# Float16 pairs in place of float32r pairs for the feed-forward and for attention's queries and keys

## The chip, the cores and the metric

The kernel runs on one core of a Trainium2 chip. The metric is the device time of one execution in microseconds (us). The kernel before took 3118.67 us (median of three runs, 3118.27 to 3121.66). One more execution was recorded by the hardware profiler; it took 3119.8 us, and the span from its first to its last instruction is 3117.9 us.

## The reference

One layer of a diffusion transformer, in float32, over 2048 tokens of width 1024, with 256 context tokens. Cut to its core:

```python
h  = modulate(rmsnorm(x,  norm1_g), sh1,  sc1)       # 2048 x 1024
hc = modulate(rmsnorm(xc, norm1_g), csh1, csc1)      # 256 x 1024
rq, rk, rv, rg, aq, ak, av = split(h @ w_in)         # widths 512 512 512 512 512 128 128
ret = ret_out(bidir_retention(rope(rq), rope(rk), rv), rg)           # 4 heads, chunks of 128
q = rope(rmsnorm(aq, q_norm_g)); k = rope(rmsnorm(ak, k_norm_g))     # 8 query heads, 2 key heads, width 64
att = softmax(q @ [k_ctx, k].T * 64**-0.5) @ [v_ctx, v]              # 2304 keys
x = x + g1 * (concat[ret, att] @ w_out)
h2 = modulate(rmsnorm(x, norm2_g), sh2, sc2)
x = x + g2 * (square(relu(h2 @ w_ff1)) @ w_ff2)      # 1024 -> 4096 -> 1024
out = rmsnorm(x, final_norm_g)
```

The shifts, scales and gates (`sh1`, `sc1`, `g1`, `sh2`, `sc2`, `g2`) are the six parts of `silu(c) @ w_mod + b_mod`.

## The kernel before, in words

Tiles have 128 partitions. Engines: PE multiplies, and PEld loads PE's stationary operand; DVE (VectorE), ACT (ScalarE) and POOL (GpSimd) compute; SP issues most DMAs. PE's wide products are made as pairs: an operand is split into a high part and a low part (`hi = cast(x)`, `lo = x - hi`), and a product is three matmuls (hi hi, hi lo, lo hi) into one PSUM bank. Before the change nearly all pairs are in float32r, a 4-byte form; the softmax numerators (`phi`, `plo`) and the values (`wv`) are in float16.

**First stage** (the `with ExitStack() as st` block). The 18 tiles of tokens go through in three groups of six; for each group six column chunks of `w_in` are multiplied (`products`, L690 to L692). Beside it run the modulation (`w_mod` is read; L306 and `later_rows`, L338 and L340), the rotary embeddings and norms of queries and keys (`post`), and stores of all results to DRAM scratch. Here Tile's scheduler sets the order of the instructions on each engine; an engine then runs its own list strictly in that order. SP's list holds nearly all loads and stores of the stage. A tile pool with `bufs=n` holds n buffers, so load number n + 1 of that pool waits until the first buffer has been read. Near the end `first_maximum` begins the first attention group (PE `mp`, DVE `nm`).

**Attention** (`Group`, run by `attention`) is under an order written out by hand: a table of events by step and phase. There are 32 groups (16 tiles of 128 queries, two key heads, four query heads each), and 18 steps for each, one per 128 keys. In a step PE makes the scores `st` (L179 with the high parts of the queries, L180 with the low parts and two extra rows that carry minus the row's maximum), one piece of the next group's maxima `mp` (L143, L147), and every second step 16 products with the values (`o`, L212 and L213). DVE takes the maxima (`nm`, L156), ACT the exponential (`p`, L185) and its float16 cast (`phi`, L189), DVE or POOL the low part (`plo`). Queries come from the scratch `aq` as float32 and are copied to float32r by ACT (L130, L133). Steps have room on PE beside that: up to about 1030 us the **retention** runs there, afterwards the **output projection** (L1146 to L1148) and the second norm.

**Feed-forward** (from about 1660 us). Two halves of 1024 tokens; for each half 16 blocks of 256 hidden units. A block makes `pu` (L1348 to L1350), squares its relu (`up_out`), and adds `pd` (L1365 to L1367) into `acc` (L1368). `w1` and `w2` come by DMA, `w2` is multiplied by the gate `g2b` on POOL (L1318), and both are split by ACT (L64) and DVE (L65).

Of the kernel before, what the change touches and what calls it, by code (L numbers as in the profile page):

```python
# [11 lines left out]
F32 = mybir.dt.float32  # L12
# [10 lines left out]
P = 128  # L23
# [13 lines left out]
PSHIFT = 8  # L37
VW = 2 * HD + 1
# [14 lines left out]
def layer_kernel(ctx: ExitStack, tc: tile.TileContext, a: dict, out: bass.AP):  # L53
# [12 lines left out]

    half = const.tile([P, 8], F32, name="half")
# [10 lines left out]
    def scratch(name, n, shape):  # L78
        return [dram.tile(shape, F32, name=f"{name}{i}", tag=f"{name}{i}") for i in range(n)]
# [4 lines left out]
    aq_d = scratch("aq", NT, [P, 2, 4, P])  # L84
# [5 lines left out]
    vm_d = dram.tile([P], F32, name="vm", tag="vm")  # L90
    h2_d = scratch("h2", NT, [P, KT, P])
# [7 lines left out]

    keep = ctx.enter_context(ExitStack())  # L100
    kp = keep.enter_context(tc.tile_pool(name="kp", bufs=1, reuse_waits="tile"))
    ks = kp.tile([P, 2, NK * P], F32R, name="ks")
# [9 lines left out]
    class Group:  # L112
# [7 lines left out]
        def load(self, pool=None, tag="q32", bufs=1):  # L120
            self.q = (pool or qp).tile([P, 2, 4, P], F32, name="q32", tag=tag, bufs=bufs)
            for e in range(2):
                src = aq_d[self.t][64 * e : 64 * e + 64, :, 2 * self.g : 2 * self.g + 2]
                q = self.q.rearrange("p x (j e) t -> p x j e t", e=2)
                nc.sync.dma_start(q[:64, :, :, e], src)
                nc.sync.dma_start(q[64:, 0, :, e], src[:, 0])

        def convert(self, pool=None, tag="qr", bufs=3):
            self.qr = (pool or qp).tile([P, 2, 4, P], F32R, name="qr", tag=tag, bufs=bufs)
            nc.scalar.activation(self.qr[:, 0], self.q[:, 0], AF.Copy)  # L130

        def convert_low(self):
            nc.scalar.activation(self.qr[:64, 1], self.q[:64, 1], AF.Copy)  # L133
# [35 lines left out]
        def rows(self):  # L169
            nc.scalar.activation(self.qr[64:, 1], self.m[64:], AF.Copy)  # L170

        def rows2(self):
            nc.vector.tensor_tensor(self.qr[96:, 1], self.m[96:], f32(self.qr[96:, 1]), op=ALU.subtract)
# [8 lines left out]
        def exp(self, kt):  # L182
            if kt % 2 == 0:
                self.p[kt // 2] = pp.tile([P, 2, 512], F32, name="p32", tag="p32")
            nc.scalar.activation(self.p[kt // 2][:, kt % 2], self.s.pop(kt), AF.Exp, bias=shift)  # L185
# [58 lines left out]
    with ExitStack() as st:  # L244
# [203 lines left out]

        def rope(dst, x, c, s, h, d, add_eng):
# [36 lines left out]
        def post(col, kind, i, ps):  # L486
# [39 lines left out]
            elif col == C_AQ:  # L526
# [3 lines left out]
                nc.vector.tensor_scalar_mul(r, r, HD ** -0.5)  # L530
# [5 lines left out]
                def turn(y=y):  # L536
# [3 lines left out]
                    qh = op.tile([P, 4, P], F32R, name="qh", tag="t1")  # L540
                    nc.scalar.activation(qh, pt, AF.Copy)
                    ql = op.tile([P, 4, P], F32, name="ql", tag="t2")
                    nc.vector.tensor_tensor(ql, pt, f32(qh), op=ALU.subtract)
# [1040 lines left out]
```

## Time and profile before

| | |
|---|---|
| time, median of three | 3118.67 us |
| profiled execution: time, span | 3119.8 us, 3117.9 us |
| PE busy, share, matmuls | 2979.0 us, 96%, 17524 |
| DVE busy, share | 1830.9 us, 59% |
| ACT busy, share | 1358.9 us, 44% |
| POOL busy, share | 1267.9 us, 41% |
| HBM read, written | 227.23 MB, 64.10 MB |

A matmul's recorded duration reaches over the starts of its successors, because matmuls are pipelined: a 128x512 matmul is recorded with 390 ns while the next starts 227 ns after it. So PE counts as busy when a matmul is in flight, and what a matmul costs in a dense stream is read from start to start. The granted clock was 0.991 of full speed over the whole span.

### The profile page before, as it was taken

What the parts mean: (1) busy time and instruction counts of PE and PEld (TensorE: products, weight loads), DVE (VectorE), ACT (ScalarE), POOL (GpSimd) and SP (SyncE); (2) the same over time, 40 slices, a digit from 0 to 9 for tenths busy, and PEclk for the clock granted to TensorE, in tenths of its full rate; (3) what the DMA queues carried; (4) which work ended last, traced back from release to release, by engine and by line L of the source; (5) the groups of instructions that cost most, each with busy time, mean ns of one, the idle gap of its engine ahead of it and who ended that gap; (6) DMA issues with size and microseconds to landing.
All of it is one profiled execution on the core that took longest, in us unless ns stands there. A gap on an engine that the chain in (4) does not pass through costs nothing.

```text
span 3117.9 us, 45735 instructions
## 1 busy us (share of the span) xinstructions
PE 2979.0 (96%) x17524; PEld 2419.4 (78%) x17524; DVE 1830.9 (59%) x2939; ACT 1358.9 (44%) x2186; POOL 1267.9 (41%) x1044
## 2 busy tenths in 40 slices
PE   7899998999888899999999999999999999999998
PEld 4787786877776677777777788888887788888886
DVE  4758466368888776677673544444444544444444
ACT  3433244257777777777776222222223222212222
POOL 3547165157777555555555222212224222222222
PEclk9999999999999999999999999999999999999999
DMA  8756544244333221222114311111114311111111
GB/s 265 218 189 194 182 137 134 83 144 141 102 116 92 67 74 63 69 74 69 64 41 161 106 48 49 53 48 43 53 48 138 112 51 51 48 48 48 48 51 54
DMA packets 202611, 294.33 MB, mean 94 GB/s; under 512 B 22932, under 2 KB 104852, under 8 KB 202392
## 3 DMA queue, kind: packets, MB, share of 16 engines
q1 hardware_dynamic: 192112, 283.92, 28.0%
q10 hardware_dynamic: 10280, 7.48, 0.8%
q8 instruction: 138, 2.26, 0.3%
q14 instruction: 81, 0.66, 0.1%
HBM read 227.23 MB, written 64.10 MB: 93 GB/s over the span
## 4 chain that ended last, share of the span: by engine, by line
PE 72%; DVE 9%; POOL 3%; ACT 3%; DMA 3%; issue 2%; SPq 0%; DVEq 0%; ACTq 0%; POOLq 0%
PE pd L1365 7%; PE pd L1367 7%; PE pd L1366 7%; PE pu L1349 7%; PE pu L1348 7%; PE pu L1350 7%; PE st L179 3%; PE st L180 3%; PE mp L143 3%; PE o L213 3%; PE pso L690 2%; PE pso L691 2%; PE pso L692 2%; PE bank L1146 2%; DVE nm L156 2%
## 5 line engine op out<-in xcount | busy, mean ns | idle before, releaser
L1355 POOL TENSOR_TENSOR r<-r 128x512 f32<-128x512 f32 x128 | 134.9, 1054 | 1000.2 <-ACT r L1354 1000.2
L156 DVE TENSOR_REDUCE nm<-mp 128x1 f32<-128x512 f32 (+1 forms) x576 | 393.2, 687 | 228.6 <-PE mp L143 188.4
L185 ACT ACTIVATE p<-st,shift 128x512 f32<-128x512 f32 x576 | 392.8, 689 | 204.7 <-PE st L180 148.7
L1368 DVE TENSOR_TENSOR acc<-pd,acc 128x512 f32<-128x512 f32 x512 | 346.6, 689 | 209.8 <-PE pd L1367 201.9
L196 POOL TENSOR_TENSOR plo<-p,phi 128x1024 f16<-128x1024 f32 x160 | 363.8, 2274 | 255.5 <-ACT phi L189 227.1
L1365 PE MATMUL pd<-w2hi,uhi 128*128 128x512 f32 x1024 | 400.6, 391 | 12.2 <-DVE acc L1368 12.2
L65 DVE TENSOR_TENSOR ulo<-r,uhi 128x512 fp32r<-128x512 f32 x128 | 112.7, 880 | 492.3 <-ACT uhi L64 492.3
L1366 PE MATMUL pd<-w2lo,uhi 128*128 128x512 f32 x1024 | 399.8, 390 | 0.0
L1348 PE MATMUL pu<-h2hi,w1hi 128*128 128x512 f32 x1024 | 398.5, 389 | 1.2 <-ACT h2hi L64 1.2
L1367 PE MATMUL pd<-w2hi,ulo 128*128 128x512 f32 x1024 | 399.5, 390 | 0.0
L1349 PE MATMUL pu<-h2lo,w1hi 128*128 128x512 f32 x1024 | 398.5, 389 | 0.9 <-POOL h2lo L65 0.9
L1350 PE MATMUL pu<-h2hi,w1lo 128*128 128x512 f32 x1024 | 398.3, 389 | 0.0
L64 ACT ACTIVATE w2hi<-ws 128x512 fp32r<-128x512 f32 x128 | 77.8, 630 | 596.1 <-PE pd L1367 521.0
L189 ACT ACTIVATE phi<-p 128x1024 f16<-128x1024 f32 x288 | 303.7, 1054 | 0.0
L690 PE MATMUL pso<-whi,hi_l 128*128 128x512 f32 (+1 forms) x768 | 290.0, 379 | 0.3 <-ACT hi_l L64 0.3
L692 PE MATMUL pso<-whi,lo_l 128*128 128x512 f32 (+1 forms) x768 | 289.2, 377 | 0.1
L691 PE MATMUL pso<-wlo,hi_l 128*128 128x512 f32 (+1 forms) x768 | 289.1, 377 | 0.0
L179 PE MATMUL st<-qr,ks 128*128 128x512 f32 x576 | 266.9, 463 | 1.2 <-ACT p L185 0.6
L143 PE MATMUL mp<-ks,qr 128*128 128x512 f32 x512 | 213.0, 416 | 44.5 <-DVE nm L156 43.7
L213 PE MATMUL o<-wv,phi 128*128 128x129 f16 x2304 | 244.2, 221 | 0.0
L212 PE MATMUL o<-wv,plo 128*128 128x65 f16 x2304 | 238.1, 195 | 3.3 <-DVE plo L198 2.6
L212 PEld LDWEIGHTS <-plo 128*128 128x128 f16 x2304 | 198.7, 98 | 54.6 <-issue 48.0
(317 smaller groups left out, 6009.4 us busy)
## 6 DMA issues: line engine op xcount, KB each, us to landing
ws<-in_w_ff SPq DMA_DIRECT2D x256, 256.0 KB, 2.7
wst<-in_w_in SPq DMA_DIRECT2D x60, 512.0 KB, 4.8
wst<-in_w_mod SPq DMA_DIRECT2D x32, 512.0 KB, 4.8
orv<-rv SPq DMA_DIRECT2D x35, 256.0 KB, 3.0
ork<-rk SPq DMA_DIRECT2D x34, 256.0 KB, 3.4
q<-aq SPq DMA_DIRECT2D x66, 128.0 KB, 3.1
wst<-in_w_mod SPq DMA_DIRECT2D x32, 256.0 KB, 4.4
x_l<-in_x SPq DMA_DIRECT2D x16, 512.0 KB, 6.1
```

Source lines behind the costliest of these rows:

```text
L156: nc.vector.tensor_reduce(dst, src, axis=AX.X, op=ALU.max, negate=True)
L179: mm(ps, ks[:, self.g, k], q[:, 0], start=True, stop=False)
L185: nc.scalar.activation(self.p[kt // 2][:, kt % 2], self.s.pop(kt), AF.Exp, bias=shift)
L196: nc.gpsimd.tensor_tensor(lo, p, hi, op=ALU.subtract)
L212: mm(o[:, : HD + 1], lo[:, i, c], v[:, : HD + 1], start=False, stop=False)
L690: mm(ps[:, :width], hi[:, k], wh, start=k == 0, stop=False)
L1348: mm(ps, whi, hi, start=k == 0, stop=False)
L1349: mm(ps, whi, lo, start=False, stop=False)
L1350: mm(ps, wlo, hi, start=False, stop=k == KT - 1)
L1365: mm(ps, uh, wh, start=f == 0, stop=False)
L1366: mm(ps, uh, wl, start=False, stop=False)
L1367: mm(ps, ul, wh, start=False, stop=f == NF - 1)
```

## The change

It has four parts.

1. The pairs of the feed-forward (`h2`, `w1`, `w2`, `u`) and attention's queries and keys (`qr`, `ks`, `ks2`) become float16. Their matmuls are as many and as large as before; a float16 operand is loaded by a LDWEIGHTS instruction of its own.
2. Powers of two keep the numbers in float16's range. For the feed-forward they come from bounds: `weight_maxima` reads all of `w_ff1` and `w_ff2` (64 tiles of 128x1024) in the first stage and takes the greatest magnitude of each tile on DVE; `ff_scales` combines them over the partitions by way of DRAM and makes the scales, which are folded into `a2` and `s2`, into the splits of `w1` (a scalar on ACT and on DVE), into the relu, into `g2b` and into the addition to `acc`. `binade` cuts a number down to its power of two. For queries and keys `balance` moves a power of two between the two norm weights.
3. The scratch `aq` holds float16, so queries are loaded as they are multiplied, and ACT's two copies for each group are gone.
4. The factor 64**-0.5 and the shift of the exponential, a scalar held in a tile before, move: the factor to the exponential's immediate scale, the shift to a third extra row of the scores.

The diff, cut to its core:

```diff
@@ Group
-        def load(self, pool=None, tag="q32", bufs=1):
-            self.q = (pool or qp).tile([P, 2, 4, P], F32, name="q32", tag=tag, bufs=bufs)
+        def load(self, pool=None, tag="qr", bufs=4):
+            self.qr = (pool or qp).tile([P, 2, 4, P], F16, name="qr", tag=tag, bufs=bufs)
...
-        def convert(self, pool=None, tag="qr", bufs=3):
-            self.qr = (pool or qp).tile([P, 2, 4, P], F32R, name="qr", tag=tag, bufs=bufs)
-            nc.scalar.activation(self.qr[:, 0], self.q[:, 0], AF.Copy)
-
-        def convert_low(self):
-            nc.scalar.activation(self.qr[:64, 1], self.q[:64, 1], AF.Copy)
...
-            nc.scalar.activation(self.p[kt // 2][:, kt % 2], self.s.pop(kt), AF.Exp, bias=shift)
+            nc.scalar.activation(self.p[kt // 2][:, kt % 2], self.s.pop(kt), AF.Exp, scale=HD**-0.5)
@@ first stage
-    ks = kp.tile([P, 2, NK * P], F32R, name="ks")
+    ks = kp.tile([P, 2, NK * P], F16, name="ks")
...
+        def weight_maxima():
+            def piece(i):
+                w = sg.tile([P, D], F32, name="wm", tag="wm", bufs=2)
+                if i < 32:
+                    src = a["w_ff1"][0, i // 4 * P : (i // 4 + 1) * P, i % 4 * D : (i % 4 + 1) * D]
+                else:
+                    src = a["w_ff2"][0, (i - 32) * P : (i - 31) * P, :]
+                nc.sync.dma_start(w, src)
+                nc.vector.tensor_reduce(wmx[:, i : i + 1], w, axis=AX.X, op=ALU.max, apply_absolute_value=True)
+
+            return [lambda i=i: piece(i) for i in range(64)]
+
+        def ff_scales():
+            x = {}
+
+            def spread():
+                w = xp.tile([P, D], F32, name="fs", tag="x", bufs=6)
+                x["m"], m = w[:, 4:516], w[:, :4]
+                nc.vector.tensor_reduce(
+                    m[:, :2], wmx.rearrange("p (a b) -> p a b", a=2), axis=AX.X, op=ALU.max
+                )
...
+                nc.sync.dma_start(sm_d, m)
+                nc.sync.dma_start(
+                    x["m"], sm_d.rearrange("p a -> (p a)").partition_broadcast(P)
+                )
+
+            def scales():
+                b = sm.tile([P, 8], F32, name="fsb", tag="fsb", bufs=1)
...
+            return [spread, scales]
...
+            if (g, c) == (2, 5):
+                spare += ff_scales()
...
+                    if maxima and (g, c) >= (1, 0):
+                        maxima.pop(0)()
@@ feed-forward
         nc.sync.dma_start(ff["g2"], gate_d[1].partition_broadcast(P))
+        m = one.tile([P, 4], F32, name="gm")
+        e, r, k = (m[:, i : i + 1] for i in range(3))
+        nc.vector.tensor_reduce(e, ff["g2"], axis=AX.X, op=ALU.max, apply_absolute_value=True)
+        binade(e)
+        nc.vector.tensor_scalar_mul(e, e, 2.0)
+        nc.vector.reciprocal(r, e)
+        nc.vector.tensor_scalar_mul(r, r, w2s)
+        nc.vector.tensor_scalar_mul(ff["g2"], ff["g2"], r)
+        nc.vector.tensor_tensor(k, sc2, e, op=ALU.mult)
+        ff["k"] = k
...
-            hi = ff["w1"].tile([P, 2, FB], F32R, name="w1hi", tag="w1hi")
-            lo = ff["w1"].tile([P, 2, FB], F32R, name="w1lo", tag="w1lo")
+            hi = ff["w1"].tile([P, 2, FB], F16, name="w1hi", tag="w1hi")
+            lo = ff["w1"].tile([P, 2, FB], F16, name="w1lo", tag="w1lo")
...
-            split(hi, lo, w.rearrange("p (k n) -> p k n", k=2))
+            w = w.rearrange("p (k n) -> p k n", k=2)
+            nc.scalar.activation(hi, w, AF.Copy, scale=sc1)
+            nc.vector.scalar_tensor_tensor(lo, w, sc1, hi, op0=ALU.mult, op1=ALU.subtract)
...
-            [ff["h"].tile([P, KT, 512], F32R, name=f"h2{x}", tag=f"h2{x}{tg}") for x in ("hi", "lo")]
+            [ff["h"].tile([P, KT, 512], F16, name=f"h2{x}", tag=f"h2{x}{tg}") for x in ("hi", "lo")]
...
-        nc.scalar.activation(r, pu.pop((f, tg)), AF.Relu)
+        nc.scalar.activation(r, pu.pop((f, tg)), AF.Relu, scale=scu)
...
-        nc.vector.tensor_tensor(acc[:, c], ps, acc[:, c], op=ALU.add)
+        nc.vector.scalar_tensor_tensor(acc[:, c], ps, ff["k"], acc[:, c], op0=ALU.mult, op1=ALU.add)
```

The scheduler makes a new order of the first stage. Three places are shown; line numbers are those of each kernel's own file.

SP's list in the first stage, before. `wst` are tiles of `w_mod` (L296) and `w_in` (L434), `x_l` tiles of tokens:

```order
L392 DMA x_l_458<-in_x 128x1024
L296 DMA wst<-in_w_mod 128x2x256 x2
L748 DMA n_291<-in_n 128x8
L434 DMA wst<-in_w_in 128x2x512
L296 DMA wst<-in_w_mod 128x2x256 x8
```

The same place after the change, where L312 is the `w_mod` load, L450 the `w_in` load and L656 the new load `wm` of a feed-forward weight tile:

```order
L847 DMA n_297<-in_n 128x8
L656 DMA wm<-in_w_ff 128x1024 x2
L450 DMA wst<-in_w_in 128x2x512
L312 DMA wst<-in_w_mod 128x2x256 x6
L656 DMA wm<-in_w_ff 128x1024 x2
L312 DMA wst<-in_w_mod 128x2x256 x2
```

And the place in the new list where the last of the 64 stands:

```order
L577 DMA aq_124<-qh 128x512
L656 DMA wm<-in_w_ff 128x1024
L450 DMA wst<-in_w_in 128x2x512
L578 DMA aq_124<-ql 128x512
L345 DMA wst<-in_w_mod 128x2x512
L656 DMA wm<-in_w_ff 128x1024
L577 DMA aq_125<-qh 128x512
```

The program text spreads the pieces over the second and third groups; in the list the first two stand ahead of the stage's second `w_in` load, and the last ahead of the store of `aq_125`, a tile of the second group.

DVE's list a little further on, before (rotary embedding of the retention's keys, then the gate's rows of `w_mod`):

```order
L455 TENSOR_TENSOR t_912<-xs,rtb 128x512
L338 TENSOR_SCALAR macc<-wst,cc 128x512
L340 SCALAR_TENSOR_TENSOR macc<-wst,cc,macc 128x512
L462 TENSOR_TENSOR ys<-t_912,t_913 128x512
L340 SCALAR_TENSOR_TENSOR macc<-wst,cc,macc 128x512 x2
L455 TENSOR_TENSOR t_957<-xs,rtb 128x512
```

The same place after, with L657 the maximum of one weight tile:

```order
L489 TENSOR_TENSOR t_902<-xs,rtb 128x512
L657 TENSOR_REDUCE wmx<-wm 128x1
L496 TENSOR_TENSOR ys<-t_902,t_903 128x512
L657 TENSOR_REDUCE wmx<-wm 128x1
L354 TENSOR_SCALAR macc<-wst,cc 128x512
L489 TENSOR_TENSOR t_928<-xs,rtb 128x512
```

Each maximum waits for its load and stands between operations on which ACT and PE depend.

PE's list in a step of attention beside the output projection, before:

```order
L213 MATMUL o_15209<-wv,phi 128x129
L179 MATMUL st<-qr,ks 128x512
L180 MATMUL st<-qr,ks_6226 128x512
L143 MATMUL mp<-ks,qr 128x512
L1146 MATMUL bank_15204<-sf_8485,oat 128x512
```

And after:

```order
L229 MATMUL o_15371<-wv,phi 128x129
L195 LDWEIGHTS ks
L195 MATMUL st<-qr,ks 128x512
L196 LDWEIGHTS ks_6449
L196 MATMUL st<-qr,ks_6449 128x512
L158 LDWEIGHTS qr
L158 MATMUL mp<-ks,qr 128x512
L1250 MATMUL bank_15366<-sf_8689,oat 128x512
```

The matmuls stand in the same order; the float16 ones have their weight loads as rows of their own.

More of the change, by code (lines that the diff above doesn't have):

```diff
@@ L75, in rsqrt, with scratch @@
         return y
-    def scratch(name, n, shape):
-        return [dram.tile(shape, F32, name=f"{name}{i}", tag=f"{name}{i}") for i in range(n)]
+    def scratch(name, n, shape, dtype=F32):
+        return [dram.tile(shape, dtype, name=f"{name}{i}", tag=f"{name}{i}") for i in range(n)]
     rk_d = scratch("rk", NK, [P, 512])
@@ L90, in layer_kernel @@
     vm_d = dram.tile([P], F32, name="vm", tag="vm")
+    sm_d = dram.tile([P, 4], F32, name="smd", tag="smd")
     h2_d = scratch("h2", NT, [P, KT, P])
@@ L447, in layer_kernel, with balance @@
         gnb = one.tile([P, 512], F32, name="gnb")
+        def balance(g):
+            m = sm.tile([P, 4], F32, name="gm", tag="gm", bufs=1)
+            nc.vector.tensor_reduce(
+                m[:, :2], g.rearrange("p a b c -> p a (b c)"), axis=AX.X, op=ALU.max, apply_absolute_value=True
+            )
+            nc.vector.tensor_scalar_max(m[:, :2], m[:, :2], 1e-15)
+            nc.vector.reciprocal(m[:, 2:3], m[:, 0:1])
+            nc.vector.tensor_mul(m[:, 2:3], m[:, 2:3], m[:, 1:2])
+            e = m[:, 2:3].bitcast(I32)
+            nc.vector.tensor_single_scalar(e, e, 24, op=ALU.arith_shift_right)
+            nc.vector.tensor_scalar(e, e, 8388608.0, float(64 << 23), op0=ALU.mult, op1=ALU.add)
+            nc.vector.reciprocal(m[:, 3:4], m[:, 2:3])
+            for i in range(2):
+                nc.vector.tensor_scalar_mul(g[:, i], g[:, i], m[:, 2 + i : 3 + i])
         def rope(dst, x, c, s, h, d, add_eng):
@@ L753, in layer_kernel @@
         mods = mod_steps()
+        maxima = weight_maxima()
         beside = None
@@ L817, in layer_kernel @@
     psX = pool(banks, "psX", space=PSUM, side="right")
-    ks2 = vp.tile([P, 2, NK * P], F32R, name="ks2")
+    ks2 = vp.tile([P, 2, NK * P], F16, name="ks2")
     unit = vp.tile([P, 1], F32, name="unit")
     nc.vector.tensor_tensor(unit, ident[:, 64:65], ident[:, 96:97], op=ALU.add)
-    shift = vp.tile([P, 1], F32, name="shift")
-    nc.vector.memset(shift, PSHIFT * math.log(2.0))
+    nc.vector.tensor_tensor(unit, unit, ident[:, 80:81], op=ALU.add)
+    nc.vector.tensor_scalar_mul(unit, unit, ROW)
     zeros = vp.tile([P, P], F16, name="zeros")
@@ L1334, in make_h @@
         hi, lo = (x[:, 4 * q : 4 * q + 4, j % 4 * P : (j % 4 + 1) * P] for x in ff["hs"][j // 4])
[L1335 removed]
+        split16(hi, lo, ff.pop(("u", i)), eng or (nc.vector if i % 2 else nc.gpsimd))
     UP = [(f, tg) for tg in range(2) for f in range(NF)]
@@ L1353, in up_out @@
         r = ff["r"].tile([P, 512], F32, name="r", tag="r")
-        nc.scalar.activation(r, pu.pop((f, tg)), AF.Relu)
+        nc.scalar.activation(r, pu.pop((f, tg)), AF.Relu, scale=scu)
         nc.gpsimd.tensor_tensor(r, r, r, op=ALU.mult)
-        us[f, tg] = [ff["up"].tile([P, 512], F32R, name=f"u{x}", tag=f"u{x}") for x in ("hi", "lo")]
-        split(*us[f, tg], r)
+        us[f, tg] = [ff["up"].tile([P, 512], F16, name=f"u{x}", tag=f"u{x}") for x in ("hi", "lo")]
+        split16(*us[f, tg], r)
     def down(b, m, n, acc):
```

81 lines of the change are left out of this document (59 added, 22 removed).

## The prediction

> **What bounds the kernel now.** I read the windows first, one per stage (times are from the span's start; 605 to 1030 us is attention beside the retention, 1030 to 1660 us attention beside the output projection, the last is the feed-forward).
>
> ```profile
> core 0: us, PE busy (x) PEld busy (x) DVE busy (x) ACT busy (x) POOL busy (x), PEclk, DMA share, GB/s
> 0.00:29.00 29.00, 13.18 (x49) 3.56 (x50) 6.51 (x16) 9.93 (x17) 6.64 (x18) 1.00 0.92 308
> 29.00:290.00 261.00, 248.99 (x1324) 197.94 (x1323) 183.09 (x305) 96.86 (x177) 138.84 (x162) 0.99 0.64 203
> 605.00:1030.00 425.00, 370.78 (x3149) 305.90 (x3147) 343.81 (x662) 291.11 (x456) 295.94 (x214) 0.98 0.37 117
> 1030.00:1660.00 630.00, 618.51 (x5228) 489.13 (x5227) 435.83 (x739) 502.57 (x757) 323.54 (x218) 1.00 0.19 62
> 1660.00:3118.00 1458.00, 1427.29 (x6338) 1177.13 (x6335) 687.02 (x938) 351.86 (x601) 381.50 (x308) 0.99 0.20 67
> ```
>
> PE is busy 98% of the feed-forward and of the projection's stretch, with the next engine at 47% and 80%. Only beside the retention does PE have time to spare (87%), and DVE is close behind it (81%). PE's waits agree: over 3118 us the longest entries are small.
>
> ```profile
> PE mp L143 <- DVE nm L156: 43.7, 42, 2.6
> PE pd L1365 <- DVE acc L1368: 12.2, 6, 3.8
> ```
>
> Nearly all of the first fall into 605 to 1030 us. So elsewhere the time is the number of matmuls times the distance from one start to the next, and a dearer operation on another engine is free while that engine has room.
>
> **Matmul spacing, the change's main term.** The feed-forward's dense stream, its first and last row of 22 (columns: start, duration, engine, line, operation):
>
> ```profile
> 2201.23 0.39 PE L1365 MATMUL pd<-w2hi,uhi 128*128 128x512 f32 x1
> ...
> 2205.99 0.39 PE L1365 MATMUL pd<-w2hi,uhi 128*128 128x512 f32 x1
> ```
>
> 21 distances in 4.76 us are 226.7 ns for 512 columns. The profile has no wide float16 matmul; the nearest are these, first a block of two with 258 columns, then the first and last of eight pairs with 65 and 129:
>
> ```profile
> 971.17 0.39 PE L204 MATMUL o<-wv,zeros 128*128 128x258 f16 x2
> 971.39 0.19 PE L212 MATMUL o<-wv,plo 128*128 128x65 f16 x1
> ...
> 1304.21 0.22 PE L213 MATMUL o<-wv,phi 128*128 128x129 f16 x1
> ...
> 1304.82 0.22 PE L213 MATMUL o<-wv,phi 128*128 128x129 f16 x1
> ```
>
> Two of 258 columns take 0.22 us, 110 ns each; seven pairs take 0.61 us, 87 ns for 194 columns, or 43.6 ns for a mean of 97. The line through both has (110 − 43.6)/161 = 0.412 ns per column and gives 110 + 254 × 0.412 = 214.7 ns at 512. The float32r rows of 256 columns give another slope:
>
> ```profile
> 80.73 0.28 PE L691 MATMUL pso<-wlo,hi_c 128*128 128x256 f32 x1
> ...
> 82.15 0.28 PE L691 MATMUL pso<-wlo,hi_c 128*128 128x256 f32 x1
> ```
>
> Twelve distances in 1.42 us are 118.3 ns, so (226.7 − 118.3)/256 = 0.423 ns per column, and 110 + 254 × 0.423 = 217.5. I take the middle, 216.5 ns: a float16 matmul saves 10.2 ns, 4.5%. The narrow pairs carry their own weight loads at 44 ns distance, so the added load instructions cost nothing here. Rounding to 10 ns leaves 105 to 115 ns for the 258 columns, hence 211.5 to 221.5 and a saving of 5 to 15 ns.
>
> The feed-forward has 2 × 16 × 64 × 3 = 6144 such matmuls, as this group (one of its six lines, 1024 each) shows:
>
> ```profile
> L1365 PE MATMUL pd<-w2hi,uhi 128*128 128x512 f32 x1024 | 400.6, 391 | 12.2 <-DVE acc L1368 12.2
> ```
>
> 6144 × 10.2 = **−63 us** (bounds −31 to −92). The additions to `acc`, the relu and the splits of `w1` get scalars from tiles. They lie on DVE and ACT: if each of DVE's 938 instructions there took half as long again, DVE would be busy 1031 of 1458 us, so they stay hidden under PE. Without that cover the additions (one row below, 512 of them) at 0.1 us more would cost 51 us.
>
> ```profile
> L1368 DVE TENSOR_TENSOR acc<-pd,acc 128x512 f32<-128x512 f32 x512 | 346.6, 689 | 209.8 <-PE pd L1367 201.9
> ```
>
> The Trainium skill, "TensorE: Matmul & The Clock Gate", section "Wait — 56ns, not 53.3ns?", gives 215.7 ns from start to start for a warm 512-column matmul, which I estimate at 6144 × 11.0 = 68 us saved here, 5 more than my term. The 226.7 ns of this trace are more than that page's figure, and no run here yet shows a wide float16 matmul.
>
> **Attention beside the output projection.** PE is full there, so what it saves is gained. A float32r matmul after a float16 one is dearer: L179 follows the products with the values, L180 follows L179.
>
> ```profile
> L179 PE MATMUL st<-qr,ks 128*128 128x512 f32 x576 | 266.9, 463 | 1.2 <-ACT p L185 0.6
> L180 PE MATMUL st<-qr,ks 128*128 128x512 f32 x576 | 231.1, 401 | 0.0
> ```
>
> The handover is 463 − 401 = 62 ns. After the change the first matmul behind the products is float16 too, and the handover is moved, if it stays, to the projection's matmuls, which already follow maxima or scores. The stretch has this many scores and, in the second row, maxima:
>
> ```profile
> 1030.00:1660.00 630.00, 259.30 (x753) 123.13 (x752) 255.32 (x376) 1.00 0.19 62
> 1030.00:1660.00 630.00, 130.00 (x320) 60.16 (x319) 1.00 0.19 62
> ```
>
> 376 steps × (2 × 10.2 + 62) = 31.0, and 320 × 10.2 = 3.3: **−34 us**. Lower bound of the gain 0 (the handover moves to the projection's matmuls and the spacing stays), upper 40 with 15 ns. I take the sum, since the projection's float32r matmuls come in runs of several, of which a handover meets one.
>
> **Attention beside the retention.** DVE paces it with POOL:
>
> ```profile
> 650.00:1030.00 380.00, 328.72 (x2958) 272.01 (x2958) 331.61 (x641) 276.31 (x434) 283.07 (x202) 0.98 0.39 122
> 650.00:1030.00 380.00, 142.04 (x390) 62.33 (x390) 133.33 (x194) 0.98 0.39 122
> DVE mr L1000 <- POOL cy_gn L863: 24.9, 16, 2.8
> DVE nm L156 <- PE mp L143: 16.2, 19, 1.3
> ```
>
> PE's saving is 194 × 82.4 ns = 16 us, but PE has 51 us idle. DVE waits for PE 16.2 us; a third of that, since its other waits stay, is **−6 us** (bounds 0 and −16).
>
> **ACT in attention.** The exponential no longer reads its shift from a tile, and the copies of the queries go.
>
> ```profile
> L185 ACT ACTIVATE p<-st,shift 128x512 f32<-128x512 f32 x576 | 392.8, 689 | 204.7 <-PE st L180 148.7 <-DVE plo L198 43.6 <-POOL plo L196 9.0
> L522 ACT ACTIVATE xs<-pso 128x512 f32<-128x512 f32 x16 | 9.6, 598 | 37.6 <-PE pso L692 37.5
> L130 ACT ACTIVATE qr<-q 128x512 fp32r<-128x512 f32 x33 | 20.8, 631 | 5.9 <-DMA q<-aq 5.9
> L133 ACT ACTIVATE qr<-q 64x512 fp32r<-64x512 f32 x33 | 20.6, 625 | 0.0
> ```
>
> Up to 576 × (689 − 598) ns = 52 us and 41 us leave ACT. It waits 148.7 us for the scores already, and is idle 127 us beside the projection: **0** (bounds 0 and −16, a shorter chain from scores to products). The float16 queries and keys are written by operations that exist already.
>
> **First stage.** 64 loads of 512 KB and 64 maxima of 128x1024 are added. The nearest maximum and the nearest load, of the same size and rows, and how long that load takes from issue to landing (least, median, most):
>
> ```profile
> L590 DVE TENSOR_REDUCE vma<-vn x3: 937/941/954, 460.8 to 465.3; 128x1 f32<-128x768 f32 x3
> x_l<-in_x SPq DMA_DIRECT2D x16, 512.0 KB, 6.1
> DMA to landing us min/median/max: 3.9/6.0/9.1
> 1698.37 0.14 DVE L1166 TENSOR_TENSOR ss<-ss 128x1 f32<-128x1 f32 x1
> ```
>
> The last row gives a DVE operation's fixed part; 1024 columns take 0.14 + 0.80 × 1024/768 = 1.21 us. In the changed order the pieces stand from the stage's second `w_in` load to just ahead of the store of `aq_125`:
>
> ```profile
> 28.82 0.37 SPq L434 DMA_DIRECT2D wst<-in_w_in  x1
> 282.55 0.32 SPq L544 DMA_DIRECT2D aq<-qh  x1
> ```
>
> so they fall into 29 to 290 us. DVE's busy time there becomes 183.1 + 64 × 1.21 = 260.5 of 261 us. The DMA engines carry 0.64 × 261 = 167 us; 33.6 MB more, at 308/0.92 = 335 GB/s in full use, add 100: 267 of 261 us. Both resources that had room are used up, while every maximum waits for its load and PE waits for DVE's rotary, norm and split operations queued behind it. An engine with such dependences has not run fuller than DVE's 331.6/380 = 87% beside the retention: 260.5/0.87 = 299 us, a stretch of 38; DMA at the 0.92 of the first 29 us gives 290, a stretch of 29. I take **+37 us**, near DVE's. Bounds: 0, if the order fills DVE's gaps, and 77, if every maximum lies on the path. SP's list is one queue, and each `wm` load also holds up the `w_in` and token loads behind it until a buffer is free.
>
> **Small chains.** `ff_scales` stores, reloads and computes on DVE, like the existing round trip: **+3 us** (bounds 0 and 7). Before the feed-forward `g2b` is reduced by eight DVE operations after its landing: **+1 us** (bounds 0 and 5), since PE has projection work left.
>
> ```profile
> DVE vma L599 <- DMA vma<-vm: 6.7, 1, 6.7
> DMA to landing us min/median/max: 5.9/5.9/5.9
> ```
>
> **The sum:** −63 − 34 − 6 + 37 + 3 + 1 = −62, on the profiled 3119.8 us: 3058, and 1.1 less against the median of 3118.67, so **3057 us**.
>
> **Rivals.**
>
> *The maxima hide.* DVE's 78 idle us before the change take 77 us of maxima, and the stage grows by 5 at most: 3057 − 32 = 3025. For it: one scheduler places them by need; against it: DVE would have to run at 98%. The Trainium skill, "DMA: Bandwidth & Descriptors", section "Measured (HBM→SBUF, 128 partitions, SWDGE, issued from GpSimd)", has 425 GB/s for 16 MB; I estimate 79 us for the added bytes by it, which would leave the DMA engines at 246 of 261 us and speak for this rival. No stretch of this trace moves more than 308 GB/s.
>
> *A landing loop, the slower side.* `wm` has two buffers, so two loads, their landing and two maxima make a round, 32 rounds in all, and SP's other loads queue behind them. At 6.1 us of landing a round is 6.1 + 1.2 + 0.7 (two issues) = 8.0 us and 32 make 256, just within the 261. With the DMA engines full the landing will be later: at the longest seen, 9.1 us, they make 352, +91 instead of +37: 3111. From 9.4 us per landing on (361 us) the loss equals the other gains of 99 us; at 10.5 us it is 397, +136: 3156. For it: the sixteen loads took up to 9.1 us at a DMA share of 0.64. Against: not all `wm` loads stand next to other traffic.
>
> *More from attention.* Relieved of the copies and the exponential's scalar, ACT and PE let the retention's steps come sooner, up to the bound of 16 us each beside the 6 counted: −20 more, 3037.
>
> *No gain per wide matmul.* The 226.7 ns could stay, if float16's advantage is one of narrow matmuls. Only the handover is left, 376 × 62 = 23: −23 − 6 + 41 = +12, 3131. Against: the slope per column is the same in both types, so the fixed part is what differs.
>
> **Chances.** Forecast 0.50, maxima hidden 0.22, more from attention 0.12, landing loop 0.12 (two thirds of it slower than before), no gain per wide matmul 0.04. Faster by over 0.2% (6 us, about what a measurement of this kernel can tell): 0.50 + 0.22 + 0.12 and a little of the loop, less the forecast's tail, 0.84; within 0.2% 0.05; slower 0.11. The range reaches from a little under the hidden case, with a spacing 2 ns better than taken (3012), to the loop at 9.1 us (3111).
>
> **What would show it.** Starts of L1365's successors 216 to 217 ns apart in the feed-forward, and that stage 63 us shorter (1395); the mean of the first scores' matmul down by about 60 ns more than the second's; 1030 to 1660 us shorter by 34; DVE above 85% and a DMA share above 0.85 in the first 330 us, the first stage's end (605 us) 37 to 40 us later, and waits of the weight maxima for `wm`. It is wrong if wide float16 matmuls keep 227 ns, if the granted clock in the feed-forward falls (each 0.01 of it is 14 us), if DVE's waits for `wm` exceed 60 us, or if the first stage ends within 10 us of before.

## The result

The changed kernel took 3046.72 us (median of four runs, 3040.09 to 3050.60), beside 3118.84 us for the kernel before on the same chips: a ratio of 0.9765 (95% interval 0.9746 to 0.9783), 72 us or 2.3% faster. The forecast was 3057 us, with a range of 3012 to 3111.

The profiled execution took 3047.53 us, its span is 3045.7. The windows of the profile after, with the boundaries used before (columns: window, length, busy time and count of each engine, granted clock of PE, DMA share, GB/s):

```profile
29.00:290.00 261.00, 244.71 (x1278) 194.36 (x1277) 225.54 (x333) 91.69 (x167) 124.16 (x147) 0.98 0.89 304
290.00:605.00 315.00, 294.92 (x1409) 238.07 (x1408) 192.92 (x323) 109.37 (x184) 135.86 (x135) 0.98 0.49 154
605.00:1030.00 425.00, 364.11 (x3186) 278.21 (x3185) 339.35 (x657) 260.33 (x429) 291.80 (x215) 0.98 0.34 108
1030.00:1660.00 630.00, 606.16 (x5386) 410.13 (x5385) 454.06 (x760) 462.32 (x737) 344.02 (x228) 0.99 0.19 60
1660.00:3045.00 1385.00, 1351.93 (x6224) 615.93 (x6224) 712.87 (x940) 362.48 (x589) 369.22 (x304) 0.99 0.21 70
```

Between 29 and 290 us the DMA share went from 0.64 to 0.89, DVE's busy time from 183 to 226 us, and PE started 46 matmuls fewer in the same time. Between 1030 and 1660 us PE's busy time fell from 619 to 606 us and ACT's from 503 to 462; in the feed-forward PE's fell with the length of the stage and ACT's rose, from 352 to 363 us.

Fixed windows cut a shifted kernel at other places, so the stages are better measured between marks of the program on PE: the last product of the first stage, the first product of the output projection, the feed-forward's first and last matmul. The mark on which most of what follows rests is the last product. Its row before, and then its row after (columns: start, duration, engine, line, operation):

```profile
644.81 0.39 PE L692 MATMUL pso<-whi,lo_l 128*128 128x512 f32 x1
```

```profile
663.03 0.39 PE L791 MATMUL pso<-whi,lo_l 128*128 128x512 f32 x1
```

Lengths in us, from the timelines of the profiled executions (one for each kernel; the changed kernel and the one below with the feed-forward in float32r again have the same program in the first stage, and their marks at its end are 663.0 and 666.5 us, so that a few us between single marks mean nothing):

| | before | after | change | forecast |
|---|---|---|---|---|
| start to the first stage's last product | 644.8 | 663.0 | +18.2 | +37 and +3 |
| from there to the projection's first product (retention) | 401.4 | 395.8 | −5.6 | −6 |
| from there to the feed-forward's first matmul | 645.8 | 621.4 | −24.4 | −34 |
| feed-forward, first to last matmul | 1414.1 | 1353.7 | −60.4 | −63 and +1 |
| rest of the span | 11.8 | 11.8 | 0 | 0 |
| span | 3117.9 | 3045.7 | −72.2 | −62 |

### The profile page after: what moved, and what is told of

The parts are those of the page before. It is cut to its first block, busy times and chain, and to the rows that moved or that the text cites. A ratio compares the mean times of both kernels' runs of the same rounds, so it can differ in the third digit from the quotient of the medians.

```text
span 3045.7 us, 45858 instructions
## 1 busy us (share of the span) xinstructions
PE 2874.4 (94%) x17524; PEld 1740.0 (57%) x17524; DVE 1932.4 (63%) x3035; ACT 1295.5 (43%) x2120; POOL 1271.7 (42%) x1046
## 4 chain that ended last, share of the span: by engine, by line
PE 69%; DVE 14%; DMA 6%; POOL 4%; issue 4%; ACT 2%; SPq 0%; ACTq 0%; DVEq 0%; POOLq 0%
PE pd L1482 7%; PE pd L1484 7%; PE pd L1483 7%; PE pu L1467 7%; PE pu L1465 7%; PE pu L1466 7%; PE o L229 3%; PE st L196 3%; PE st L195 3%; PE mp L158 3%; PE pso L789 3%; DVE nm L171 2%; PE pso L791 2%; PE pso L790 2%; PE bank L1250 2%
## 5 line engine op out<-in xcount | busy, mean ns | idle before, releaser
L1485 DVE SCALAR_TENSOR_TENSOR acc<-pd,gm,acc 128x512 f32<-128x512 f32 x512 | 373.7, 746 | 154.0 <-PE pd L1484 153.8
L201 ACT ACTIVATE p<-st 128x512 f32<-128x512 f32 x576 | 340.7, 598 | 249.2 <-PE st L196 174.5
L1482 PE MATMUL pd<-w2hi,uhi 128*128 128x512 f16 x1024 | 390.0, 381 | 14.1 <-DVE acc L1485 13.9
L1466 PE MATMUL pu<-h2lo,w1hi 128*128 128x512 f16 x1024 | 388.7, 380 | 2.6 <-POOL h2lo L71 2.6
L1465 PE MATMUL pu<-h2hi,w1hi 128*128 128x512 f16 x1024 | 388.9, 380 | 1.2 <-ACT h2hi L70 1.2
L1483 PE MATMUL pd<-w2lo,uhi 128*128 128x512 f16 x1024 | 389.9, 381 | 0.0
L1484 PE MATMUL pd<-w2hi,ulo 128*128 128x512 f16 x1024 | 389.7, 381 | 0.1
L1467 PE MATMUL pu<-h2hi,w1lo 128*128 128x512 f16 x1024 | 388.7, 380 | 0.0
L158 PE MATMUL mp<-ks,qr 128*128 128x512 f16 x512 | 196.7, 384 | 55.8 <-DVE nm L171 55.6
L214 DVE TENSOR_TENSOR plo<-p,phi 128x512 f16<-128x512 f32 x256 | 214.4, 839 | 19.2 <-ACT phi L205 19.1
```

Of the source, the lines that this page charges most:

```text
L1465: mm(ps, whi, hi, start=k == 0, stop=False)
L1466: mm(ps, whi, lo, start=False, stop=False)
L1467: mm(ps, wlo, hi, start=False, stop=k == KT - 1)
L1482: mm(ps, uh, wh, start=f == 0, stop=False)
L1483: mm(ps, uh, wl, start=False, stop=False)
L1484: mm(ps, ul, wh, start=False, stop=f == NF - 1)
```

## Experiments

The time of each kernel is the median of its runs; its ratio is to runs of the kernel before on the same chip. "Last product" is the mark above, read from the profiled execution.

### The feed-forward in float32r again

```diff
-            hi = ff["w1"].tile([P, 2, FB], F16, name="w1hi", tag="w1hi")
+            hi = ff["w1"].tile([P, 2, FB], F32R, name="w1hi", tag="w1hi")
...
-        split16(*us[f, tg], r)
+        split(*us[f, tg], r)
```

and so for `w1lo`, `w2`, `h2` and `u`.

> The changed kernel with the feed-forward's pairs (h2, w1, w2, u) in float32r again; scales, maxima and attention as changed. If the spacing of 216 against 227 ns is the feed-forward's whole gain, its products (first to last) take 1414 us as before the change in place of 1354, and the time is 3047 + 60 = 3107. Rival: a part of it comes from the new order or from DVE and ACT there; then the stage takes 1395 us or less and the time is 3090 or less.

It took 3114.26 us, ratio 0.9974 (0.9965 to 0.9983). The feed-forward's marks lie 1417.6 us apart, 63.9 more than after the change and 3.5 more than before it; the stages ahead of it were as after the change (666.5, 395.1 and 623.9 us). So the feed-forward's operand type is worth 64 us of the 72 and the rest of the change together about 8. The dense stream shows why. After the change, the first and last of 22 rows:

```profile
2200.54 0.38 PE L1465 MATMUL pu<-h2hi,w1hi 128*128 128x512 f16 x1
...
2205.07 0.38 PE L1465 MATMUL pu<-h2hi,w1hi 128*128 128x512 f16 x1
```

21 distances in 4.53 us are 215.7 ns; in float32r they were 226.7. 6144 × 11.0 would be 68 us; 4 to 7 of them went to longer stalls (the longest, for `acc`, 5.6 us).

### The exponential's shift from a tile again

```diff
-            nc.scalar.activation(self.p[kt // 2][:, kt % 2], self.s.pop(kt), AF.Exp, scale=HD**-0.5)
+            nc.scalar.activation(self.p[kt // 2][:, kt % 2], self.s.pop(kt), AF.Exp, scale=HD**-0.5, bias=shift)
```

with the third extra row of the scores left at zero.

> The changed kernel with the shift of the exponential read from a tile again, as before the change, and not in the scores' third row: the mean of the exponential should go from 598 back to 689 ns, 52 us on ACT. By the prediction's step (ACT bounds nothing) the time stays: 3047 within 4 us. Rival: the 7 us gained beside the retention, or a part of the 23 beside the projection, come from the shorter exponential; then 3053 to 3063, with the loss between 668 and 1680 us.

It took 3050.57 us, ratio 0.9773 (0.9759 to 0.9786), which can't be told from the changed kernel's 0.9765. The groups of ACT, first after the change, then in this experiment:

```profile
L201 ACT ACTIVATE p<-st 128x512 f32<-128x512 f32 x576 | 340.7, 598 | 249.2 <-PE st L196 174.5 <-DVE plo L214 60.6 <-POOL plo L212 6.4
```

```profile
L201 ACT ACTIVATE p<-st,shift 128x512 f32<-128x512 f32 x576 | 391.9, 689 | 211.2 <-PE st L196 141.0 <-DVE plo L214 55.4 <-POOL plo L212 8.4
```

The same instruction with the same scale costs 91 ns more for the pointer. Of the 51 us taken from ACT, 38 turn up as idle time ahead of it; the retention's stage (397.7 us) and the projection's (621.3) stay within 2 us of the changed kernel's.

### No maxima

```diff
-        maxima = weight_maxima()
+        maxima = []
+        nc.vector.memset(wmx, 0.25)
```

> The changed kernel without the 64 loads and the 64 maxima of the feed-forward weights; the greatest magnitudes are a constant 0.25 in their place, so that part of the computation is left out. In the changed kernel the last product of the first stage starts at 663.0 us of the span, before the change at 644.8. If the maxima alone stretch the stage, it starts at 643 to 648 us here and the time is 3047 - 18 = 3029 us. Rival: the new order, the scales and the float16 queries and keys cost the 18 us; then it stays at 655 us or later and the time at 3038 or more.

It took 3022.93 us, ratio 0.9683 (0.9670 to 0.9696). The last product:

```profile
639.42 0.39 PE L791 MATMUL pso<-whi,lo_l 128*128 128x512 f32 x1
```

23.6 us ahead of the changed kernel and 5.4 ahead of the kernel before. So the loads and maxima cost some 24 us in the changed kernel, and the other edits of the first stage, or merely the other order that the scheduler finds, gave 5 back (which of the two is not shown).

### Loads alone

```diff
-                nc.vector.tensor_reduce(wmx[:, i : i + 1], w, axis=AX.X, op=ALU.max, apply_absolute_value=True)
+                nc.vector.tensor_reduce(wmj[:, i : i + 1], w[:, :1], axis=AX.X, op=ALU.max, apply_absolute_value=True)
...
+        nc.vector.memset(wmx, 0.25)
```

> The changed kernel with its 64 loads, but each maximum over one column (about 0.14 us, an estimate from a 128x1 operation of the trace, in place of 1.21) and the constant 0.25 for the scales; most of DVE's added 77 us is left out. If DVE's time stretches the first stage (the step of the prediction), the last product starts at 645 to 650 us and the time is about 3031. Rival, the DMA engines (share 0.94 between 29 and 140 us) and SP's one queue: it stays at 658 to 663 us and the time at 3042 to 3047.

It took 3038.73 us, ratio 0.9736 (0.9722 to 0.9749), and the last product starts here:

```profile
657.13 0.39 PE L792 MATMUL pso<-whi,lo_l 128*128 128x512 f32 x1
```

With hardly any of DVE's work, 17.7 of the 23.6 us are still there. This speaks against the step of the prediction that made DVE's pace the cause. It leaves open whether the loads cost by what they carry or by the places where engines wait for them: DVE still stands before loads that have not landed, for 36.2 us in all.

### Maxima alone, and maxima alone but spread

First the maxima over a tile that never changes:

```diff
-                nc.sync.dma_start(w, src)
-                nc.vector.tensor_reduce(wmx[:, i : i + 1], w, axis=AX.X, op=ALU.max, apply_absolute_value=True)
+                nc.vector.tensor_reduce(wmx[:, i : i + 1], wr, axis=AX.X, op=ALU.max, apply_absolute_value=True)
```

> The changed kernel with its 64 maxima of 128x1024 over a tile that lies in the chip's memory and holds 0.25; the 64 loads (33.6 MB) are left out. If DVE's time stretches the first stage, the last product starts at 658 to 663 us and the time is 3042 to 3047. Rival, DMA and SP's queue: 645 to 650 us and about 3031. If both are needed together, both of these halves come out near 648.

It took 3068.45 us, ratio 0.9828 (0.9815 to 0.9841), with the last product at 685.5 us: later than with the loads, which neither theory had. The reason is in the order. With nothing to wait for, the scheduler put all 64 at the head of DVE's list (columns of the second row as in the windows above):

```profile
L655 DVE TENSOR_REDUCE wmx<-wr x64: 1200/1204/1219, 2.9 to 87.0; 128x1 f32<-128x1024 f32 x64
0.00:95.00 95.00, 34.43 (x174) 15.08 (x175) 90.32 (x110) 15.95 (x26) 11.65 (x27) 0.75 0.55 178
```

DVE is busy 90 of the first 95 us, and PE, which waits for the operations queued behind the maxima, 34. The run says nothing on the cause in the changed kernel, only that 64 maxima in one block ahead of everything else cost 46 us against none. So a second form holds each maximum back behind a product of the second or third group:

```diff
-                nc.sync.dma_start(w, src)
-                nc.vector.tensor_reduce(wmx[:, i : i + 1], w, axis=AX.X, op=ALU.max, apply_absolute_value=True)
+                nc.vector.tensor_copy(wr[:, :1], after)
+                nc.vector.tensor_reduce(wmj[:, i : i + 1], wr, axis=AX.X, op=ALU.max, apply_absolute_value=True)
...
-                        maxima.pop(0)()
+                        maxima.pop(0)(ps[:, :1])
```

> The counterpart of the paced kernel without its loads: 64 maxima of 128x1024 over a tile that holds 0.25, each behind a copy of one column of a product of the second or third group, so that they are spread as there (the last product started at 660.0 us) and can't be put ahead of all other work; the scales come from the constant 0.25, and the 33.6 MB are left out. If DVE's added 77 us stretch the stage, the prediction's step, the last product starts at 655 to 661 us and the time is 3038 or more. If the bytes do, it is 641 to 648 us (639.4 without any maxima, and the 6 us that DVE added to the loads) and the time 3024 to 3031.

It took 3016.63 us, ratio 0.9657 (0.9644 to 0.9670): faster than without any maxima. The maxima's group, the last product, and a window in the thick of them:

```profile
L653 DVE TENSOR_REDUCE wmj<-wr 128x1 f32<-128x1024 f32 x64 | 77.6, 1212 | 1.0
632.76 0.39 PE L787 MATMUL pso<-whi,lo_l 128*128 128x512 f32 x1
224.00:330.00 106.00, 102.50 (x506) 82.09 (x505) 101.88 (x160) 38.67 (x69) 64.24 (x71) 1.00 0.60 186
```

DVE's 77.6 us are all there, DVE runs at 96% for 106 us, and PE runs at 97% beside it at full clock. Spread like this, DVE's time by itself stretches nothing. That the stage ends 6.6 us sooner than with no maxima, though it has more work, shows what a new order from the scheduler can do; differences of that size between these kernels are not to be read as costs. The loads' cost stands clear of it: of the kernels with float32r there, this one, the one without maxima and the one that has them elsewhere end the stage at 632.8 to 639.4 us, and the six with all loads in it at 657.1 to 666.5.

### The same spread with loads

```diff
+                nc.vector.tensor_copy(w[:, :1], after)
...
-                    if maxima and (g, c) >= (1, 0):
-                        maxima.pop(0)()
+                    for _ in range(1):
+                        if maxima and (g, c) >= (1, 0):
+                            maxima.pop(0)(ps[:, :1])
```

> The changed kernel with all its work; each of the 64 loads waits for a product of the second or third group (a copy of one column into its tile ahead of the load), one load for each product, so that they are spread from about 225 us to the stage's end and no two come at once by themselves. If the cost is one of density (DMA share of 0.86 to 0.94 for 200 us, in the changed kernel and in the one with late pieces), the last product starts at 645 to 650 us and the time is 3028 to 3034. Rival: the loads cost some 18 us however they are spread: 657 us or later, 3041 or more.

It took 3039.38 us, ratio 0.9735 (0.9722 to 0.9749). The last product, the window above and DVE's longest wait of this kernel:

```profile
659.97 0.39 PE L792 MATMUL pso<-whi,lo_l 128*128 128x512 f32 x1
224.00:330.00 106.00, 98.30 (x487) 78.89 (x486) 97.97 (x158) 38.51 (x67) 66.59 (x70) 0.98 0.78 249
DVE wmx L658 <- DMA wm<-in_w_ff: 57.0, 34, 4.8
```

Against the same spread without loads the stage ends 27 us later, at a DMA share of at most 0.80 in any window of 50 us. Density was not the point: the loads cost about the same spread over 390 us (224.7 to 613.6) as packed into 280. In this form DVE stands before a load that has not landed for 57 us; in the changed kernel for 11.5 us only, but there SP's list stands:

```profile
SPq L656 <- DVE wmx L657: 46.5, 35, 3.0
DVE wmx L657 <- DMA wm<-in_w_ff: 11.5, 11, 2.3
```

### A quarter of the bytes

```diff
-                w = sg.tile([P, D], F32, name="wm", tag="wm", bufs=2)
+                w = sg.tile([P, 256], F32, name="wm", tag="wm", bufs=2)
```

with 256 columns of each weight tile loaded, one column reduced, and the constant 0.25 for the scales as before.

> As the kernel with loads only (64 loads, each maximum over one column, the constant 0.25 for the scales), but each load brings 128x256 in place of 128x1024: 8.4 MB in all, a quarter of the bytes, with the same number of instructions on SP and DVE and the same two buffers. Without loads the last product of the first stage starts at 639.4 us, with full loads at 657.1. If the bytes cost (other loads land later), a quarter of 17.7 is left: 642 to 646 us, 3022.9 + 4 = 3027. Rival, the places in SP's queue and the waits for a free buffer there: 651 to 657 us and 3033 to 3039.

It took 3028.13 us, ratio 0.9702 (0.9689 to 0.9715), and the last product starts here:

```profile
645.60 0.39 PE L792 MATMUL pso<-whi,lo_l 128*128 128x512 f32 x1
```

The same number of instructions on SP and DVE with a quarter of the bytes costs 6.2 us instead of 17.7. The greater part of the loads' cost goes with their bytes, that is, as it seems, with how long they and the transfers beside them take to land; a rest of up to 6 us is queueing, or order. The transfers beside them do land later. The loads of `w_in`, first in the changed kernel, then without loads and maxima (the last number is the median time to landing in us):

```profile
wst<-in_w_in SPq DMA_DIRECT2D x60, 512.0 KB, 5.3
```

```profile
wst<-in_w_in SPq DMA_DIRECT2D x60, 512.0 KB, 4.6
```

It is 5.3 us too with the loads alone, 5.2 with the spread loads, and 4.8 with a quarter of the bytes.

### The maxima at other places

Later in the first stage (the first two loads wait for a product of the second group's third chunk, so that all 64 maxima fall into 296 to 533 us):

```diff
-                    if maxima and (g, c) >= (1, 0):
-                        maxima.pop(0)()
+                    for _ in range(2):
+                        if maxima and (g, c) >= (1, 2):
+                            maxima.pop(0)(ps[:, :1] if len(maxima) > 62 else None)
```

> The changed kernel with all its work; the first two of the 64 loads wait for a product of the second group's third column chunk (a copy of one column into their tile ahead of the load), and the program calls two pieces at each place from there. So the 64 pieces fall into about 300 to 580 us, where the DMA share was 0.45 and DVE busy 55% before the change. If the stretch comes from the place, where both had no room, the last product starts at 646 to 652 us and the time is 3030 to 3036. Rival: the same work costs the same anywhere in the stage: 660 us or later, 3044 or more.

3042.85 us, ratio 0.9749 (0.9735 to 0.9762), last product at 659.1 us: the rival, nearly. And beside the output projection:

```diff
-        maxima = weight_maxima()
+        maxima = []
...
+        for i in range(64):
+            k = 190 + 6 * i
+            on(k, "dma", load, i)
+            on(k + 5, "late", greatest, i, 0)
+            on(k + 5 + 1, "late", greatest, i, 1)
+        on(576, "late", spread)
+        on(576 + 6, "late", scales)
```

> The changed kernel with the 64 loads and maxima taken out of the first stage and put beside the output projection: one load of 512 KB every six steps into one buffer, two maxima of 128x512 behind it, and the weights' scales computed after the last one; the scales of the second norm stay in the first stage. Nothing is left out. The DMA share there is 0.19 and DVE busy 72%. If the bytes cost in the first stage alone because transfers there are awaited, the last product starts at 639 to 642 us, the projection's stretch stays at 621 us and the time is 3023 to 3027. Rival: DVE's 64 x 1.3 us delay the row maxima there and PE waits: the stretch grows to 632 us or more and the time is 3034 or more.

3043.32 us, ratio 0.9749 (0.9736 to 0.9763). The first stage went back to 639.1 us, as without maxima, but the projection's stretch grew from 621.4 to 640.0. The loads landed in good time there (DVE was idle 0.3 us ahead of all 128 maxima), and DVE was busy 82% of the stretch. The maxima's group, and one of ACT's waits in that stretch:

```profile
L1330 DVE TENSOR_REDUCE wmx<-wm 128x1 f32<-128x512 f32 x128 | 86.5, 676 | 0.3
ACT p L203 <- DVE plo L216: 33.5, 20, 2.5
```

The same wait in the changed kernel, over its stretch:

```profile
ACT p L201 <- DVE plo L214: 2.9, 5, 1.7
```

So DVE's later low parts hold up ACT, and ACT the scores. Set matmul for matmul beside the changed kernel, some 11 of the 18.6 us lost come in many small delays on PE up to 1600 us. The other 7 come in the last 77 us of the stretch, where PE waits 8.3 instead of 5.6 us for the second norm (`u`, on DVE) and the granted clock is 0.89 instead of 0.96. The waits point to DVE here; no run separates its time from the loads' bytes. So of three places and one spread, the 64 loads and maxima cost some 19 to 24 us of the stage they stand in.

### More pairs in float16

The first stage's products and the output projection's, unscaled:

```diff
-                hi = hp.tile([P, KT, P], F32R, name=f"hi_{kind}{i}", tag="hhi")
+                hi = hp.tile([P, KT, P], F16, name=f"hi_{kind}{i}", tag="hhi")
...
-            hi = wp.tile([P, 2, 512], F32R, name="whi", tag="whi")
+            hi = wp.tile([P, 2, 512], F16, name="whi", tag="whi")
...
-            x = room_tile(tag, F32R)
+            x = room_tile(tag, F16)
```

> The changed kernel with two more sets of pairs in float16, unscaled: the first stage's products (hidden states and w_in) and the output projection's (w_out times the gate, and what it multiplies). It asks what paces the first stage after the change. The stage has 2064 products of 512 columns and 384 of 256; at 10.6 and about 8 ns less that is 25 us. If PE's spacing paces it, the last product starts near 638 us in place of 663. Rival: the added loads pace it; then it stays at 655 us or later. For the projection the distances of the changed kernel (scores' successor and L1250 to L1251 together 446 ns, 232 and 239 ns behind the others) say 255 x 52 ns = 13 us if every one becomes 216: the stretch from the first projection product to the feed-forward's first goes from 621 to about 608 us. Together 3009 us, by the rival 3026 to 3034.

It took 3012.80 us, ratio 0.9651 (0.9637 to 0.9664), the fastest kernel here that leaves nothing out: another 34 us. The projection's stretch went from 621.4 to 607.7 us, 13.7 less, as worked out from starts (13). The first stage's last product went from 663.0 to 644.7, 18 of the 25 us that the spacing alone would give; by that PE's spacing would still pace a good part of the first stage, but this kernel's order is a new one too, and the next kernel does not bear it out.

With the maxima beside the projection as well:

> Both of the other two edits together: maxima beside the output projection, and the first stage's and the projection's pairs in float16 as well. If the first stage without the loads is paced by PE's spacing, the last product starts near 640 - 25 = 615 us and the time is 3025 - 38 = 2987. Rival: DVE or the transfers of the stage itself hold it: 625 us or later and 3000 or more.

3020.93 us, ratio 0.9678 (0.9665 to 0.9692), with the last product at 630.8 us and the projection's stretch at 627.4. What the two edits do doesn't add up: without loads the first stage gained 8 of the 25 us (639.1 to 630.8), which is not far above the scatter of the order, and the projection's stretch lost 20 against the kernel with maxima in the first stage. What holds the first stage then is open.

## Why the prediction was right, and where it was not

The sum was −62 and the profile shows −72. Two of its terms were off, with opposite signs: the projection's gain was put 10 us too high, the first stage's loss 22 us too high. That the total came within 10 us is in part luck.

**Matmul spacing: right.** The prediction took 216.5 ns from two lines through narrow rows (their middle, of 214.7 and 217.5, is 216.1, which would have made the term −65); the wide float16 matmul takes 215.7. The Trainium skill's figure ("TensorE: Matmul & The Clock Gate", "Wait — 56ns, not 53.3ns?"), 215.7 ns, is what this trace shows. The term came out at −60.4, since stalls took a few us back; with the feed-forward in float32r again the stage grew by 63.9. The relu, the splits and the additions with scalars from tiles did stay hidden: the additions went from 689 to 746 ns, DVE from 687 to 713 us, and the waits for them on PE from 12.2 to 13.9.

```profile
L1485 DVE SCALAR_TENSOR_TENSOR acc<-pd,gm,acc 128x512 f32<-128x512 f32 x512 | 373.7, 746 | 154.0 <-PE pd L1484 153.8
L1482 PE MATMUL pd<-w2hi,uhi 128*128 128x512 f16 x1024 | 390.0, 381 | 14.1 <-DVE acc L1485 13.9 <-ACT uhi L70 0.2
```

**Attention beside the projection: mechanism right, size off.** The step that failed is "376 steps × (2 × 10.2 + 62)": the handover of 62 ns was taken from recorded durations (463 − 401) and given to every step. The sign that the prediction named did come, the means fell to 385 and 384 ns, but some half of that was no time, as the starts show. Read from starts, before the change and then after:

```profile
1304.82 0.22 PE L213 MATMUL o<-wv,phi 128*128 128x129 f16 x1
1304.85 0.48 PE L179 MATMUL st<-qr,ks 128*128 128x512 f32 x1
1305.16 0.39 PE L180 MATMUL st<-qr,ks 128*128 128x512 f32 x1
```

```profile
1304.65 0.22 PE L229 MATMUL o<-wv,phi 128*128 128x129 f16 x1
1304.71 0.38 PE L195 MATMUL st<-qr,ks 128*128 128x512 f16 x1
1304.92 0.38 PE L196 MATMUL st<-qr,ks 128*128 128x512 f16 x1
```

From the last product with the values to the second scores it was 0.34 us (median of the start distances 27 + 319 ns) and is 0.27 (56 + 215): 75 ns less, of which about 11 are spacing. So the handover behind the products is real and about of the size taken. But a part of the longer recorded duration is an early start (27 against 56 ns after the product) and no time, and only 186 of the stretch's some 370 steps have products straight ahead of the scores. 54 more have transposes there and gained 26 ns in the mean; behind the projection's matmuls (94 steps) the two distances made 465 ns before and after. Summed over starts, the pairs of scores gave 17 us; what follows the scores and the maxima gave the other 7. The handover to the projection's float32r matmuls behind a wide float16 one, on which the lower bound rested, is free:

```profile
1306.22 0.38 PE L158 MATMUL mp<-ks,qr 128*128 128x512 f16 x1
1306.25 0.58 PE L1250 MATMUL bank<-sf,ogate 128*128 128x512 f32 x1
1306.67 0.39 PE L1251 MATMUL bank<-sf,ogate 128*128 128x512 f32 x1
```

The float32r matmul is recorded 28 ns after the maximum and with 0.58 us, but the next one starts 418 ns later (medians of 223): 446 ns for both, about the 216 + 232 of a float16 and a float32r distance without any handover. The prediction knew that products come every second step, and should have counted who follows whom.

**Retention: the number right, the reason not shown.** −5.6 us against −6. The gain builds up over the stage, but DVE's waits for `mp`, of which the prediction took a third, fell by 2 us only, from 17.4 (22 times) to 15.0 (20 times, without one of 16.7 us that begins before the stage's mark). So the agreement is partly luck.

**ACT: right.** The experiment with the pointer shows 0 within 2 us a stage. The rival "more from attention", put at 20 us more (its two bounds of 16 us, less the 6 counted, make 26), did not come.

**First stage: right sign, wrong cause.** The step that failed is "An engine with such dependences has not run fuller than DVE's 331.6/380 = 87% beside the retention: 260.5/0.87 = 299 us". DVE ran at 96% for 106 us without holding PE up, once its operations waited for no load. The maxima by themselves, where they are spread, cost nothing that can be told from the scheduler's own scatter of 6 us; the loads do (17.7 us alone, 27 at an equal spread; with a quarter of the bytes 6.2). The other term that the text had worked out, DMA at 0.92 of its time (+29), was nearer: the share became 0.89 (0.94 up to 140 us) and the stretch was 23.6 against the kernel without maxima. But full DMA engines are not the whole of it, since the spread loads cost as much at a share of at most 0.80. The prediction held that no stretch moves more than 308 GB/s; that was the highest of its windows by stage, and windows of 10 us before the change reach 366. The value taken, +37, stood near DVE's end; and the rest of the stage became 5 us shorter, which the sum did not have. The rival in which SP's queue becomes a landing loop was seen in small: `wm` loads landed after 5.5 us in the median (9.6 at most) and SP waited 46.5 us for their buffers; it made no loop that lasts as long as the stage. Which share of the loads' cost is SP's queue, the later landing of `w_in` and of the stores that ACT waits for, or DVE standing before a load, was not separated: more buffers would have shown the first, and that was not tried.

**Small chains:** +3 and +1 can't be seen apart from the scatter of the order.

## What to carry to other kernels

Where PE is full, read what a matmul costs from start to start, of the pair that stands there, and count who follows whom; a mean duration holds an early start as if it were time. When an edit adds reads beside work, ask for their bytes and who waits for the transfers already there before asking for the engine that handles them: in the first stage here 78 us on an engine with room cost nothing by themselves, as long as they were spread, and with their 33.6 MB of loads they cost some 20 us wherever they were put. And before a small difference is read as a cost, compare it with what a mere reshuffle by the scheduler does, at least 6 us here.

## What the runs showed of the hardware beside that

A wait of PE can cost more than its length. In the changed kernel PE stands still from 339.1 to 343.4 us. The granted clock (the third column from the right) in stretches around this gap and around a later one of 2.2 us, from 919.0 us:

```profile
337.50:340.90 3.40, 0.63 (x4) 1.00 0.93 312
340.90:347.70 6.80, 4.32 (x10) 0.50 0.84 281
917.80:921.20 3.40, 1.18 (x20) 1.00 0.01 2
921.20:924.60 3.40, 3.40 (x13) 0.50 0.55 192
```

After the first gap the clock is at half for 6.8 us, after the second for 3.4. In 4.3 of the 6.8 us PE has work, so the gap of 4.3 us costs about 2.1 us more (estimated as half of that time). The Trainium skill ("TensorE: Matmul & The Clock Gate", "What's actually happening") has the clock fall to half after an idle window of about 3.4 us. The lengths at half clock fit such a window, but here the window need not be wholly idle: in the 3.4 us before the clock fell PE was busy for 0.63 us in one case and 1.18 us in the other. Such slow stretches are a part of how late transfers became lost time in the first stage: ahead of the first gap ACT's `xs` had waited 3.5 us for a store (`kt<-zs`), and PE waited for `xs`.

A float16 weight load takes half as long as one in float32r, first before, then after the change:

```profile
L1365 PEld LDWEIGHTS pd<-w2hi,uhi 128*128 128x128 f32 x1024 | 192.8, 188 | 55.0 <-DVE acc L1368 15.2
```

```profile
L1482 PEld LDWEIGHTS <-uhi 128*128 128x128 f16 x1024 | 100.5, 98 | 122.0 <-issue 1.9 <-ACT uhi L70 0.6
```

PEld's share of the feed-forward fell from 81% to 44%. It lay beside the matmuls before as after, so the distance of the matmuls shows only the 11 ns.
